# Output projection beside an attention: a tile of weights between two and two modulation tiles, split half a group ahead of its use

## The chip, the cores and the metric

The kernel runs on one core of a Trainium2 chip. The metric is device time in microseconds (us) of one launch. Before the change the median of three runs is 2190.3 us (2189.67 to 2194.18).

## What is computed

Two transformer blocks run one after the other on 256 tokens of width 2048, all in float32. The change lies in the first block, between its attention and its output projection:

```python
sh_a, sc_a, g_a, sh_m, sc_m, g_m = ada_modulation(c, w_ada, b_ada)   # silu(c) @ w_ada + b_ada, six pieces of 2048
h = modulate(rms_norm(x, norm_attn_w), sh_a, sc_a)
q, k, v, u = split_projection(h @ w_in)           # 16 query heads, 4 key heads of 64
attn = latent_window_attention(q, k, v, kc, vc, sink)
pool = multiscale_pool(u, pool_w, pool_scale)
x = x + g_a * (concat([attn, pool]) @ w_out)      # w_out: 2048 x 2048
hm = modulate(rms_norm(x, norm_mlp_w), sh_m, sc_m)
x = x + g_m * (square(relu(hm @ w_up)) @ w_down)
```

The pooled half of the concatenation (rows 1024 to 2047 of w_out) is ready before the attention; the attention's half comes later.

## The kernel before

**Split matmuls.** Every weight tile (512 rows by 512 columns, 1 MB) is loaded into a tile `raw` and split in two halves of 256 rows. For each half ACT rounds it to `wh` (line 65, called at line 174) and DVE subtracts to get the rest `wl` (line 68). A product is then three matmuls of 512 columns, `mm3` (lines 237 to 239): hi by wh, hi by wl, lo by wh. One half of a tile serves four mm3 (two k-slices by two blocks of 128 tokens).

**The list of units.** Loads and what follows them stand in one list in program order: `items` (what to load) and `units` (what to do with it). A weight tile is two units (its halves); a tile of w_ada (128 rows by 2048 columns, also 1 MB, kind `an`) is one unit: eight matmuls in the trace of line 203, which add its part of the modulation vector into the bank `adab`. `prep()` (line 161) does the next unit. `ahead(n)` (line 222) does up to n units, as long as fewer than three halves are split ahead of use and the next unit isn't held: with `state["hold"]` set, units from that number on are done by `ahead` only if they are weight halves. `take(i, h)` (line 228) gives out a half, and does units until it is there. Five `raw` tiles exist in this stage (three of `raw_p`, two extra); the load of an item starts when the item five places earlier has been used up.

**The stage.** The pooled half of the output projection is eight groups, (n, g) for n = 0..3 (512 output columns) and g = 2, 3 (512 rows). One group uses one tile: two halves, each with j = 0, 1, each with t = 0, 1, so eight mm3. Between them stand pieces of the attention: `beside(w)` (line 88) adds w to a due and steps the generator `attn1` (line 807) for each whole one. attn1 has 32 units u (one head pair member and one block of 128 queries). A unit's steps are, in the order of the program:

- scores of u: three matmuls into a bank `s` (lines 815 to 818; DVE: row maximum `mx`, line 820, and `negm`, line 821; ACT: exponential into `p`)
- in every odd unit, values of the two units before: sixteen matmuls into `o` (line 835); in every fourth unit also `esk`, `rcp`, `rw` on DVE, with a small exponential and a copy `o` on ACT
- the turn of u-1: four transposes of p into a bank `bk` (line 854), copied to `pt` by ACT (odd u) or DVE (even u, line 859)
- in every fourth unit, two transposes of rw (line 866), and DVE and ACT finish two heads (xX)

The group's loop before:

```python
for h in range(2):
    wh, wl = take(i, h, 0)
    ...
    for j in range(2):
        ahead(1)
        for t in range(2):
            mm3(...)
            beside(LP1)                  # LP1 = 1.1
        if next_kind() == "an" ...: prep(); beside(LP1 * 1.4)
while next_kind() == "an": prep(); beside(LP1 * 1.4)
ahead()
```

`ADA_POOL` (line 28) says how many w_ada tiles follow each w_out tile in the list: 6, then 4 each, the last 2. Since the next weight tile stands behind all of them, and `ahead` is held at w_ada tiles (hold is 0 in this loop), a tile's halves are split at the end of the group before, by the `ahead()` after the loop (line 913). Before the loop stands the last block of q (`in_block("q1", ...)`), which does units with no hold.

Of the kernel before, what the change touches and what calls it, by code (L numbers as in the profile page):

```python
# [24 lines left out]

CTX_AT = "q1"

FILL, ADA_IN, ADA_POOL, ADA_REST = 4, 10, (6, 4, 4, 4, 4, 4, 4, 2), 1

LP1, LAG, LAGK = 1.1, 3, 2  # L30

# [11 lines left out]
def two_blocks_kernel(ctx: ExitStack, tc: tile.TileContext, I, out: bass.AP):  # L43
# [178 lines left out]
    def ahead(n=AHEAD):  # L222
        while n and state["uw"] < min(w_used[0] + AHEAD, len(w_units)) and not (
                state["hold"] is not None and state["up"] >= state["hold"] and next_kind() != "w"):
            prep()
            n -= 1
# [8 lines left out]
    def mm3(acc, xs, wh, wl, first, last):  # L235
        hi, lo = xs
        PE.matmul(out=acc, lhsT=hi, rhs=wh, start=first, stop=False)  # L237
        PE.matmul(out=acc, lhsT=hi, rhs=wl, start=False, stop=False)  # L238
        PE.matmul(out=acc, lhsT=lo, rhs=wh, start=False, stop=last)  # L239
# [67 lines left out]
    def ada_n(n):  # L307
        for _ in range(n):
            if ada_q:
                add_direct(KINDS.pop(0) if KINDS else "an", *ada_q.popleft())  # L310
# [17 lines left out]
    def add_wo(n, g):  # L328
        wo_blk[n, g] = add_w("w", [(w_out[512 * g:512 * (g + 1), 512 * n:512 * n + 512], 0, 512)], 4, 512)

    for n in range(4):
        for g in (2, 3):
            add_wo(n, g)
            ada_n(ADA_POOL[2 * n + g - 2])
    for n in (0, 2):
        for g in (0, 1):
            for e in (0, 1):
                add_wo(n + e, g)
                ada_n(ADA_REST)
    assert not ada_q  # L340
    up_blk, down_blk, fill_unit = {}, {}, []
    for k in range(16):
# [285 lines left out]
    def in_block(nm, g, more=False):  # L628
        i = win_blk[nm, g]
        k0, n = GROUPS[g]  # L630
        who = (hx, hc) if nm == "kv" else (hx,)
        a, keys = [], []
        ws = {}
        for iw, w in enumerate(who):
            while len(w) < k0 + n:
                assert step((hp, cq)[iw])
            a += [new_acc() for _ in range(2)]
            keys += [(("kvc" if iw else nm), t) for t in range(2)]
            for h in range(2):
                if not iw:  # L640
                    ws[h] = take(i, h)
                wh, wl = ws[h]
                for j in range(n // 2):
                    for t in range(2):
                        s = slice(t * 128, (t + 1) * 128)
                        k = h * n // 2 + j
                        hi, lo = w[k0 + k]
                        mm3(a[2 * iw + t], (hi[:, s], lo[:, s]), wh[:, j], wl[:, j], k == 0, k == n - 1)
                        if more:
                            tick()  # L650
                    tick()
        for (nm_, t), ac in zip(keys, a):
            if nm_ not in proj:
                proj[nm_] = xtile("R" if nm_ in ("kv", "kvc") else "X", FP32, (128, 2, 512))
            if g == 0:
                act(proj[nm_][:, t], ac)
            else:
                V.tensor_tensor(out=proj[nm_][:, t], in0=ac, in1=proj[nm_][:, t], op=OP.add)
# [67 lines left out]
    def q_post(qb, t):  # L726
        s = slice(t * 128, (t + 1) * 128)
        rs = []
        for r in rope(proj[f"q{qb}"][:, t], 8, t, "pt"):
            rs.append(r)  # L730
            yield
        for _ in range(LAG):
            yield
        for a, r in enumerate(rs[-2:]):
            bk = bank([128, 4, 128])
            for h in range(4):
                dup_t(bk[:, h, :], r[:, h])
            q = QS[0][:, qb * 8 + 4 * a:qb * 8 + 4 * a + 4, s]
            act(q, bk)
            sub_lo(q[64:128], bk[64:128], q[64:128])  # L740
            yield
# [47 lines left out]
    QS.append(nat.tile([128, 16, 256], F32R, tag="n2", name="QS"))  # L789
    for t in range(2):  # L790
        hp.append(q_post(0, t))
    in_block("q1", LAST, True)
    while "pool" not in done:
        step(hp)
# [97 lines left out]
    for n in range(4):  # L892
        gate = None
        a = [new_acc() for _ in range(2)]
        for g in (2, 3):
            i = wo_blk[n, g]
            for h in range(2):
                wh, wl = take(i, h, 0)
                if gate is None and 2 in stored:
                    gate = gate_row(2, n)  # L900
                for j in range(2):
                    k = 4 * g + 2 * h + j
                    ahead(1)
                    for t in range(2):
                        mm3(a[t], fm(k, t), wh[:, j], wl[:, j], k == 8, k == 15)
                        beside(LP1)
                    if next_kind() == "an" and items[units[state["up"]][0]][0] == "an":
                        prep()
                        beside(LP1 * 1.4)
            while next_kind() == "an":  # L910
                prep()
                beside(LP1 * 1.4)
            ahead()
        add_gated(a, n, False, gate)
        del a

# [841 lines left out]
```

## Time and profile before

| | |
|---|---|
| median of three runs | 2190.3 us |
| the profiled execution | 2190.88 us, its span 2189.1 us |
| PE (TensorE matmul) busy | 2129.6 us, 97% of the span |
| DVE (VectorE) busy | 1221.5 us, 56% |
| ACT (ScalarE) busy | 965.8 us, 44% |
| DMA | 472.08 MB, 216 GB/s over the span |
| share of PE in the chain that ended last | 94% |

PE is the engine that works nearly all the time. What the whole-span shares hide is the stage of the attention, from about 257 to 415 us: the table of 40 slices shows PE busy 9 tenths or less there, and the clock in short stretches below full. The stage is read in the table by stretches (busy time and granted clock in each), the waits of PE (whom it waited for), and the timelines of PE, ACT and DVE (which instruction waited, and what stood ahead of it on its engine). Lines are those of the kernel before.

### The profile page before, as it was taken

To read this page: it belongs to the slowest core of one execution; us is meant where nothing else is said; L and a number is where in the kernel's file an instruction comes from. 1 tells how busy PE (TensorE), PEld (TensorE's weight loads), DVE (VectorE), ACT (ScalarE), POOL (GpSimd) and SP (SyncE) were. 2 spreads that over 40 slices of the span, in tenths; PEclk is the share of its full clock that TensorE was granted. 3 is DMA by queue.
4 is the path that set the end of the run, shared out by engine and by line. 5 is a ranking of instruction groups with operands and counts; after the bars stand their busy time and mean duration, and the time that the engine had idled before them with its cause. 6 is when DMAs were issued, how large, how long until landed. Compare 5 with 4: busy or idle time off the path is not lost.

```text
span 2189.1 us, 25717 instructions
## 1 busy us (share of the span) xinstructions
PE 2129.6 (97%) x10267; PEld 1687.2 (77%) x10267; DVE 1221.5 (56%) x1553; ACT 965.8 (44%) x1343; POOL 49.9 (2%) x90
## 2 busy tenths in 40 slices
PE   5999988999999999999999999999999999999998
PEld 3677655678888888888888887888888888888886
DVE  2455555566546656554556548746665555555554
ACT  4433333355444434443444544445544444444443
POOL 1000000010000000000001000000000000000000
PEclk9999999999999999999999999999999999999999
DMA  9988866776547867565555754554556555555553
GB/s 331 371 327 334 303 216 224 276 266 207 193 170 254 281 211 256 184 206 177 189 202 184 238 181 135 164 173 151 183 177 211 193 192 192 193 192 192 192 192 115
DMA packets 213944, 472.08 MB, mean 216 GB/s; under 512 B 8897, under 2 KB 18929, under 8 KB 204865
## 3 DMA queue, kind: packets, MB, share of 16 engines
q1 hardware_dynamic: 209312, 457.53, 61.1%
q0 software_dynamic: 4448, 12.90, 2.0%
q8 instruction: 80, 1.31, 0.2%
q14 instruction: 40, 0.32, 0.0%
q10 hardware_dynamic: 64, 0.02, 0.0%
HBM read 468.28 MB, written 4.49 MB: 216 GB/s over the span
## 4 chain that ended last, share of the span: by engine, by line
PE 94%; DVE 1%; ACT 1%; DMA 1%; issue 0%; POOL 0%; POOLq 0%; ACTq 0%; DVEq 0%
PE acc L237 28%; PE acc L238 28%; PE acc L239 28%; PE adab L203 3%; PE bk L854 1%; PE o L835 1%; PE bk L1002 1%; PE s L1253 1%; DVE wl L68 1%; DMA raw<-in_w_in_dram 1%; PE o L1296 0%; PE s L818 0%; PE bk L1197 0%; PE s L815 0%; PE bk L1343 0%; DMA raw<-in_w_ada_dram 0%
## 5 line engine op out<-in xcount | busy, mean ns | idle before, releaser
L68 DVE TENSOR_TENSOR wl<-raw,wh 128x1024 fp32r<-128x1024 f32 (+1 forms) x674 | 799.1, 1206 | 608.7 <-ACT wh L65 608.4
L65 ACT ACTIVATE wh<-raw 128x1024 fp32r<-128x1024 f32 (+1 forms) x674 | 690.3, 1043 | 526.0 <-PE acc L239 433.8
L237 PE MATMUL acc<-wh,xX 128*128 128x512 f32 x1888 | 756.9, 401 | 8.7 <-ACT wh L65 5.7
L238 PE MATMUL acc<-wl,xX 128*128 128x512 f32 x1888 | 737.9, 391 | 3.8 <-DVE wl L68 3.7
L239 PE MATMUL acc<-wh,xX 128*128 128x512 f32 x1888 | 738.6, 391 | 0.0
L237 PEld LDWEIGHTS acc<-wh,xX 128*128 128x128 f32 x1888 | 355.2, 188 | 107.5 <-issue 20.7
L239 PEld LDWEIGHTS acc<-wh,xX 128*128 128x128 f32 x1888 | 355.3, 188 | 77.3 <-DVE xX L68 0.4
L238 PEld LDWEIGHTS acc<-wl,xX 128*128 128x128 f32 x1888 | 355.9, 189 | 74.2 <-DVE wl L68 5.7
L237 PE MATMUL acc<-wh,xR 128*128 128x512 f32 x704 | 278.7, 396 | 8.0 <-ACT wh L65 8.0
L238 PE MATMUL acc<-wl,xR 128*128 128x512 f32 x704 | 275.6, 392 | 2.0 <-DVE wl L68 2.0
L239 PE MATMUL acc<-wh,xR 128*128 128x512 f32 x704 | 275.5, 391 | 0.0
L237 PEld LDWEIGHTS acc<-wh,xR 128*128 128x128 f32 x704 | 132.7, 189 | 37.1 <-ACT wh L65 8.8
L238 PEld LDWEIGHTS acc<-wl,xR 128*128 128x128 f32 x704 | 132.8, 189 | 29.4 <-DVE wl L68 3.1
L239 PEld LDWEIGHTS acc<-wh,xR 128*128 128x128 f32 x704 | 132.8, 189 | 28.0
L203 PE MATMUL adab<-raw,cst 128*32 128x512 f32 (+1 forms) x736 | 92.4, 600 | 15.8 <-DMA raw<-in_w_ada_dram 15.1
L203 PEld LDWEIGHTS adab<-raw,cst 128*32 128x32 f32 x736 | 17.6, 113 | 52.3 <-issue 27.0
L65 ACT ACTIVATE junk<-x 128x512 f32<-128x512 f32 x32 | 20.2, 631 | 66.5 <-DVE x L1097 28.7
L65 ACT ACTIVATE p<-s,negm 128x512 f32<-128x512 f32 x32 | 22.0, 688 | 61.1 <-DVE negm L821 34.7
L65 ACT ACTIVATE g<-acc,r 128x512 f32<-128x512 f32 x30 | 20.6, 690 | 55.5 <-PE acc L239 55.5
L65 ACT ACTIVATE xR<-bk 128x512 f32<-128x512 f32 (+2 forms) x26 | 13.9, 534 | 67.3 <-PE bk L1197 35.7
L820 DVE TENSOR_REDUCE mx<-s 128x1 f32<-128x512 f32 x32 | 22.1, 690 | 36.0 <-PE s L818 35.7
L65 ACT ACTIVATE r<-acc 128x512 f32<-128x512 f32 x32 | 18.8, 598 | 50.2 <-PE acc L239 39.5
(295 smaller groups left out, 1289.5 us busy)
## 6 DMA issues: line engine op xcount, KB each, us to landing
raw<-in_w_in_dram SPq DMA_DIRECT2D x151, 1024.0 KB, 5.0
raw<-in_w_ada_dram SPq DMA_DIRECT2D x88, 1024.0 KB, 6.4
raw<-in_w_mlp_up_dram SPq DMA_DIRECT2D x64, 1024.0 KB, 5.3
raw<-in_w_mlp_down_dram SPq DMA_DIRECT2D x64, 1024.0 KB, 5.0
raw<-in_w_out_dram SPq DMA_DIRECT2D x32, 1024.0 KB, 5.0
raw<-in_w_branch_dram SPq DMA_DIRECT2D x16, 1024.0 KB, 5.0
raw<-in_w_ada_dram SPq DMA_DIRECT2D x16, 512.0 KB, 8.3
raw<-in_w_in_dram SPq DMA_DIRECT2D x10, 512.0 KB, 7.3
```

The lines of the kernel that those rows point to most:

```text
L65: S.activation(out=out_, in_=in_, func=func, **kw)
L68: V.tensor_tensor(out=lo, in0=full, in1=hi.bitcast(FP32), op=OP.subtract)
L203: PE.matmul(out=accs[key][32 * j:32 * j + 32, :], lhsT=cst[:, 4 * k + j if kind == "ak" else k, :], rhs=r[:, j, :], start=k == 0, stop=k = ...
L237: PE.matmul(out=acc, lhsT=hi, rhs=wh, start=first, stop=False)
L238: PE.matmul(out=acc, lhsT=hi, rhs=wl, start=False, stop=False)
L239: PE.matmul(out=acc, lhsT=lo, rhs=wh, start=False, stop=last)
L820: V.tensor_reduce(out=mx, in_=s, axis=AX.X, op=OP.max)
L835: PE.matmul(out=ob[pair_][64 * e:64 * e + 64, 0, t, :], lhsT=vn[j][:, g * 64:(g + 1) * 64], rhs=pb[w - 1 + e][:, j, :], start=j == 0, stop ...
L854: PE.transpose(bk[:, j, :], p[:, j * 128:(j + 1) * 128], ident)
L1002: PE.transpose(bk[:, j, t * 128:(t + 1) * 128], rs[t][:, (2 * pr + j) * 128:(2 * pr + j + 1) * 128], ident)
L1253: PE.matmul(out=s[:, i, :], lhsT=QT[nm][p, h, t * 128:(t + 1) * 128], rhs=KT[nm][p, h, 0:nk], start=True, stop=True)
```

## The change

In the list of units each w_out tile of the pooled half now has two w_ada tiles ahead of it and two behind it, so four lie between two tiles (two between the first and the second). `ADA_POOL` becomes 2. The number of units after the first w_out tile is kept as `wo_units`, and `hold` is set to it before the block of q1, so that w_ada tiles behind that one are left for the groups. In the loop `ahead(1)` is called before each mm3 instead of before each pair, one w_ada tile is done after each pair, and the loop over left-over w_ada tiles and the `ahead()` at a group's end are gone. With four w_ada tiles between two weight tiles, the next tile's halves come up after two of them: before the third pair of the group (j = 0 of the second half), one half before each of its two mm3. The four w_ada tiles per group, and the total, stay. The last six w_ada tiles stand 2, 1, 1, 1, 1 behind the first tiles of the attention's half, where they stood 1 each.

```diff
-FILL, ADA_IN, ADA_POOL, ADA_REST = 4, 10, (6, 4, 4, 4, 4, 4, 4, 2), 1
+FILL, ADA_IN, ADA_POOL, ADA_REST = 4, 10, 2, 1
...
     for n in range(4):
         for g in (2, 3):
+            ada_n(ADA_POOL)
             add_wo(n, g)
-            ada_n(ADA_POOL[2 * n + g - 2])
+            if n + g == 2:
+                wo_units = len(units)
+            else:
+                ada_n(ADA_POOL)
+    ada_n(ADA_POOL)
     for n in (0, 2):
         for g in (0, 1):
             for e in (0, 1):
                 add_wo(n + e, g)
-                ada_n(ADA_REST)
+                ada_n(ADA_POOL if n + g + e == 0 else ADA_REST)
...
     for t in range(2):
         hp.append(q_post(0, t))
+    state["hold"] = wo_units
     in_block("q1", LAST, True)
...
                 for j in range(2):
                     k = 4 * g + 2 * h + j
-                    ahead(1)
                     for t in range(2):
+                        ahead(1)
                         mm3(a[t], fm(k, t), wh[:, j], wl[:, j], k == 8, k == 15)
                         beside(LP1)
-                    if next_kind() == "an" and items[units[state["up"]][0]][0] == "an":
+                    if next_kind() == "an":
                         prep()
                         beside(LP1 * 1.4)
-            while next_kind() == "an":
-                prep()
-                beside(LP1 * 1.4)
-            ahead()
         add_gated(a, n, False, gate)
         del a
```

How the order of instructions moves is shown at three places. In the names, mx, negm, p, pt, o, rw are those of the attention above; QS is the queries' tile; lines after the change are higher by 6 or 7.

**Place 1, DVE, the split of tile (1, 3).** Before, at the end of group (1, 2):

```order
L867 TENSOR_TENSOR o<-o 128x256
L68 TENSOR_TENSOR xX<-o,xX 128x256
L820 TENSOR_REDUCE mx<-s 128x1
L821 TENSOR_SCALAR negm<-mx,sink_140 128x1
L68 TENSOR_TENSOR wl<-raw,wh 128x1024 x2
L820 TENSOR_REDUCE mx<-s 128x1
L821 TENSOR_SCALAR negm<-mx,sink_140 128x1
L859 COPY pt<-bk 128x512
```

With the change, from the third pair of group (1, 2):

```order
L852 COPY rw<-rcp 128x256
L68 TENSOR_TENSOR wl<-raw,wh 128x1024
L827 TENSOR_REDUCE mx<-s 128x1
L828 TENSOR_SCALAR negm<-mx,sink_140 128x1
L68 TENSOR_TENSOR wl<-raw,wh 128x1024
L866 COPY pt<-bk 128x512
L874 TENSOR_TENSOR o<-o 128x256
L68 TENSOR_TENSOR xX<-o,xX 128x256
```

The two wl stood in a row, ahead of the maximum of the next scores; now they stand apart with one maximum between them, and the copy pt of a turn stands behind the second.

**Place 2, ACT, the same tile.** Before:

```order
L65 ACTIVATE p,psum__1919<-s,negm 128x512
L65 ACTIVATE xX<-o 128x256
L65 ACTIVATE p,psum__1919<-s,negm 128x512
L65 ACTIVATE pt<-bk 128x512
L65 ACTIVATE wh<-raw 128x1024 x2
L65 ACTIVATE p,psum__1919<-s,negm 128x512 x2
```

With the change:

```order
L65 ACTIVATE esk<-esk 128x4
L65 ACTIVATE o<-o 128x256
L65 ACTIVATE pt<-bk 128x512
L65 ACTIVATE wh<-raw 128x1024
L65 ACTIVATE p,psum__1913<-s,negm 128x512
L65 ACTIVATE wh<-raw 128x1024
L65 ACTIVATE xX<-o 128x256
L65 ACTIVATE p,psum__1913<-s,negm 128x512
```

The two wh stood in a row behind a pt; now an exponential p stands between them.

**Place 3, DVE, the split of tile (1, 2) and the first scores.** Before:

```order
L68 TENSOR_TENSOR QS<-bk,QS 64x4x128 x2
L820 TENSOR_REDUCE mx<-s 128x1
L821 TENSOR_SCALAR negm<-mx,sink_140 128x1
L820 TENSOR_REDUCE mx<-s 128x1
L821 TENSOR_SCALAR negm<-mx,sink_140 128x1
L820 TENSOR_REDUCE mx<-s 128x1
L821 TENSOR_SCALAR negm<-mx,sink_140 128x1
L68 TENSOR_TENSOR wl<-raw,wh 128x1024 x2
```

With the change, from group (0, 3):

```order
L699 TENSOR_TENSOR dup<-xX,rm 128x512 x2
L68 TENSOR_TENSOR wl<-raw,wh 128x1024
L68 TENSOR_TENSOR QS<-bk,QS 64x4x128
L68 TENSOR_TENSOR wl<-raw,wh 128x1024
L68 TENSOR_TENSOR QS<-bk,QS 64x4x128
L827 TENSOR_REDUCE mx<-s 128x1
L828 TENSOR_SCALAR negm<-mx,sink_140 128x1
L827 TENSOR_REDUCE mx<-s 128x1
```

The split came after three maxima; now its halves stand between the last parts of the queries (QS), ahead of the first maximum.

## Rows read from the trace of the kernel before

**Rows 1.** The first line of the page's chain of waits that ended last: shares of the span by engine.

```profile
PE 94%; DVE 1%; ACT 1%; DMA 1%; issue 0%; POOL 0%; POOLq 0%; ACTq 0%; DVEq 0%
```

**Rows 2.** The table by stretches, three stretches between 250 and 410 us (the last lies within the second). Columns: the stretch and its length, then busy us and instruction count of PE, PEld, DVE, ACT and POOL, then PEclk (the granted TensorE clock, 1.00 being full speed), the DMA share and GB/s.

```profile
250.00:270.00 20.00, 18.49 (x106) 10.63 (x106) 13.94 (x23) 6.08 (x9) 2.56 (x5) 1.00 0.93 335
270.00:410.00 140.00, 121.10 (x794) 76.87 (x793) 70.87 (x145) 54.08 (x116) 1.62 (x3) 0.91 0.67 227
300.00:310.00 10.00, 7.55 (x43) 4.29 (x42) 4.93 (x8) 3.31 (x6) 0.00 (x0) 0.83 0.66 214
```

**Rows 3.** The waits of PE between 250 and 440 us: who was waited for, us in total, times, longest us.

```profile
PE acc L237 <- ACT wh L65: 13.6, 6, 2.9
PE acc L238 <- DVE wl L68: 5.7, 7, 1.4
PE bk L854 <- ACT p L65: 1.0, 1, 1.0
PE o L866 <- DVE rw L845: 0.3, 1, 0.3
```

**Rows 4.** The timeline of PE. Columns: start in us, duration in us (a matmul's duration overlaps the next, so pitch is read from start to start), engine, line, operation, out<-in, shape, count, and in brackets the idle time before it with its releaser.

```profile
258.92 0.50 PE L238 MATMUL acc<-wl,xX 128*128 128x512 f32 x1 [1.43 <-DVE wl L68]
...
273.00 0.66 PE L854 MATMUL bk<-ident,p 128*128 128x128 f32 x4 [1.03 <-ACT p L65]
...
301.80 0.50 PE L237 MATMUL acc<-wh,xX 128*128 128x512 f32 x1 [1.69 <-ACT wh L65]
303.06 0.50 PE L238 MATMUL acc<-wl,xX 128*128 128x512 f32 x1 [0.76 <-DVE wl L68]
...
308.41 0.45 PE L818 MATMUL s<-xR,QS 128*128 128x512 f32 x1
...
319.99 0.39 PE L237 MATMUL acc<-wh,xX 128*128 128x512 f32 x1
...
320.68 0.60 PE L854 MATMUL bk<-ident,p 128*128 128x128 f32 x4
...
328.11 0.92 PE L854 MATMUL bk<-ident,p 128*128 128x128 f32 x4
...
332.44 0.66 PE L854 MATMUL bk<-ident,p 128*128 128x128 f32 x4
...
341.99 1.09 PE L835 MATMUL o<-pt,xR 128*64 128x128 f32 x16
343.01 0.50 PE L237 MATMUL acc<-wh,xR 128*128 128x512 f32 x1
...
343.83 0.60 PE L854 MATMUL bk<-ident,p 128*128 128x128 f32 x4
344.18 0.48 PE L237 MATMUL acc<-wh,xR 128*128 128x512 f32 x1
...
344.96 0.40 PE L815 MATMUL s<-xR,QS 128*128 128x512 f32 x1
...
345.63 1.07 PE L203 MATMUL adab<-raw,cst 128*32 128x512 f32 x8
346.63 0.66 PE L854 MATMUL bk<-ident,p 128*128 128x128 f32 x4
```

**Rows 5.** The timeline of ACT, same columns.

```profile
270.87 1.28 ACT L65 ACT_TABLE_LOAD   x1 [1.80 <-DVE negm L821]
272.16 0.69 ACT L65 ACTIVATE p<-s,negm 128x512 f32<-128x512 f32 x1
...
275.32 0.69 ACT L65 ACTIVATE p<-s,negm 128x512 f32<-128x512 f32 x1 [1.04 <-DVE negm L821]
...
276.00 1.99 ACT L65 ACTIVATE wh<-raw 128x1024 fp32r<-128x1024 f32 x2
...
300.21 0.60 ACT L65 ACTIVATE pt<-bk 128x512 f32<-128x512 f32 x1 [0.80 <-PE bk L854]
300.70 1.99 ACT L65 ACTIVATE wh<-raw 128x1024 fp32r<-128x1024 f32 x2
...
309.95 0.69 ACT L65 ACTIVATE p<-s,negm 128x512 f32<-128x512 f32 x1 [3.71 <-DVE esk L840]
...
311.31 0.60 ACT L65 ACTIVATE pt<-bk 128x512 f32<-128x512 f32 x1 [0.21 <-PE bk L854]
...
324.82 0.19 ACT L65 ACTIVATE esk<-esk 128x4 f32<-128x4 f32 x1
```

**Rows 6.** The timeline of DVE, same columns.

```profile
277.08 2.36 DVE L68 TENSOR_TENSOR wl<-raw,wh 128x1024 fp32r<-128x1024 f32 x2 [1.87 <-ACT wh L65]
...
308.90 0.69 DVE L820 TENSOR_REDUCE mx<-s 128x1 f32<-128x512 f32 x1 [1.75 <-PE s L818]
309.62 0.21 DVE L821 TENSOR_SCALAR negm<-mx,sink 128x1 f32<-128x1 f32 x1
...
325.45 0.29 DVE L845 COPY rw<-rcp 128x256 f32<-128x256 f32 x1
```

**Rows 7.** The timeline of SP's DMA issues (SPq; start in us, then the time from the first issue to the end of the last of a merged row), the issues of two tiles of w_out; and the page's line on all of w_out's loads (count, KB each, median us from issue to landing).

```profile
260.03 0.38 SPq L152 DMA_DIRECT2D raw<-in_w_out_dram  x1
...
279.47 0.38 SPq L152 DMA_DIRECT2D raw<-in_w_out_dram  x1
...
raw<-in_w_out_dram SPq DMA_DIRECT2D x32, 1024.0 KB, 5.0
```

## The prediction

> **What bounds the kernel now.** I read the page's chain of waits first: 94% of the span is PE's own work [rows 1], so time comes off only where PE stands still or runs slowly. The table by stretches shows where that is: from 270 to 410 us, the attention beside the pooled half of the output projection, PE is busy 121.1 of 140 us and the granted clock is 0.91 on the mean, while before 270 it is 1.00 [rows 2]. The waits of PE name the cause: 13.6 us in six waits for ACT's `wh`, 5.7 us in seven waits for DVE's `wl`, 1.0 us for the first exponential `p`, and 0.3 us for `rw`, which I leave as it is [rows 3]. So seven of the eight groups begin with a wait for their own tile: one short (1.43 us for wl, at 258.92), six with both parts, the least of them 1.69 + 0.76 = 2.45 us at 301.80 and 303.06 [rows 4]. Together 20.3 us.
>
> The cause is order, not supply. The tile of 276.00 was sent for at 260.03, and a w_out load takes 5.0 us at the median, so it lay there from about 265 [rows 7]; its `wh` began at 276.00, 0.68 us after the exponential that stands ahead of it on ACT began [rows 5].
>
> **The clock.** [...] After the one near 327 us, PE needs 4.33 us from the turn at 328.11 to that at 332.44; the same four kinds of work (turn, mm3, scores, w_ada tile) take 2.80 us from 343.83 to 346.63, at full clock [rows 4]. That is 1.5 us per drop. The table agrees from above: a stretch with one drop has 0.83, which is 1.7 us of 10, and 140 us at 0.91 are 12.6 us, or some seven such drops for the six waits [rows 2]. Part of that fell into idle time, so I count 7 x 1.5 = 10.5 us. The wait of 1.43 us was followed by none, its stretch is at 1.00 [rows 2, 4]; the shortest that one follows has 2.45 us. The stage loses 20.3 + 10.5 = 30.8 us.
>
> **The change, part by part.** No arithmetic is added or removed: as many w_ada tiles, w_out halves and attention steps. What moves is the place of the splits: half a group (four mm3) ahead. The seven waits for wh and wl as such go, since a half is then asked for some 9 us after it was put into the queues. But a half still stands in the queues of ACT and DVE, which also carry the attention, and what is behind it there comes later. So I followed each new split by the pitches of the rows:
>
> - PE: mm3 0.75 us (0.69 from 319.99 to 320.68, 0.82 from 343.01), turn 0.35, w_ada tile 1.0, values 1.02 [rows 4]. Scores take 0.67 ahead of a w_ada tile [rows 4]; ahead of other work, where the next starts before they end, I take 0.6. The rw transposes are taken as 0.14, two against a turn's four. These last two are estimates.
> - The last matmul of the scores to mx 0.49 (308.41 to 308.90), so 0.89 from their first, which starts 0.4 earlier (an estimate from the 0.67); mx to negm 0.72, negm to p 0.33 [rows 4 to 6].
> - p to the next ACT instruction 0.68; turn to pt 0.69; pt to wh 0.49; two wh in 1.99; wh to wl 1.08; two wl in 2.36, so 1.18 each [rows 5, 6]. A pt on DVE is taken as 0.69, like the mx of as many columns [rows 6].
>
> *Tile (1, 3), places 1 and 2.* Count from the turn of unit 4. pt 0.69, wh 1.18, wl 2.26 to 3.44. Behind that wl on DVE stands the maximum of unit 6: mx 3.4, negm 4.1, p 4.45. Behind that p on ACT stands the second wh 5.1; wl 6.2 to 7.4; and behind that on DVE the pt of unit 5, done at 8.05. The values need that pt. PE reaches them after turn, mm3, scores, mm3, turn, w_ada, rw, scores, mm3: 0.35 + 0.75 + 0.6 + 0.75 + 0.35 + 1.0 + 0.14 + 0.6 + 0.75 = 5.3. It waits **2.8 us**. Here the wait for a weight turns into a wait for a pt.
>
> *Tile (1, 2), place 3.* Counted from the last queries' transposes, ACT does wh at 0.1 and QS at 1.05, DVE wl to 2.3, QS to 3.0, mx, negm 3.7; then the table load and p at 5.3 (1.29 from the load to p), the turn at 6.1 (0.84 from p) [rows 4, 5]. PE is there after 0.35 + 1.0 + 0.6 + 0.6 + 0.75 = 3.3: **2.8 us**, where it was 1.0.
>
> *Tile (2, 3).* One exponential stands between the halves, and then esk and rw. From the scores of unit 16: mx 0.9, negm 1.6, p 1.9, wh 2.6, wl 3.7 to 4.9, mx 4.8, p 5.9, wh 6.6, wl 7.65 to 8.8, esk on ACT 9.0, rw 0.63 later (324.82 to 325.45), done 0.3 after that [rows 5, 6], so its transposes 10.0. PE's own way is 0.6 + 0.35 + 0.75 + 0.6 + 0.75 + 1.02 + 1.0 + 0.35 + 0.6 + 0.75 + 0.35 + 0.75 = 7.9: **2.1 us**.
>
> *The other four.* (2, 2): two wh in a row, two wl in a row, pt at 7.6, PE there at 7.5: 0.1 us. (3, 2): a pt between the two wl, done at 5.55 (wh 2.6, wl 3.7 to 4.9, pt 0.69) against 4.2: 1.4 us. (3, 3): a pt between the two wh, so wl to 6.35, mx 6.3, negm 7.0, pt to 7.85, against 6.8: 1.1 us. (0, 3): ahead of the attention, beside the queries' transposes: none.
>
> Sum: 2.8 + 2.8 + 2.1 + 0.1 + 1.4 + 1.1 = 10.3 us of idle. Two of these are past 2.45 us and cost a drop; 2.1 is nearer to 2.45 than to 1.43, so a third; 1.4 and 1.1 cost none: 3 x 1.5 = 4.5 us. After: 14.8 us. **Gain 30.8 - 14.8 = 16.0 us.** The profiled execution is 2190.88 us, 0.6 above the median of 2190.3; 2190.9 - 16.0 = **2175 us**. Unknown are the waits behind the queues. From below, none of them: 30.8 us gained, 2160. From above, each as dear as a wait now: nothing gained, 2191.
>
> Loads are covered: the stage moves 227 GB/s at a DMA share of 0.67; 16 us less of 140 makes 227 x 140 / 124 = 256 GB/s, against 335 at a share of 0.93 in the 20 us ahead [rows 2]. If that cover went, each microsecond of a late tile is one of PE. The moved w_ada tiles behind the attention's half stand beside full PE work before and after; the hold leaves one w_ada tile fewer in q1's block and one more in the first group, 1.0 us either way, nothing on the sum.
>
> [...]
>
> **The rivals.** *All waits go* (2160): attention instructions become ready later or the chains run shorter than I add up; the waits are 1.1 to 2.8 us, sums of five to ten pitches, and none was seen in this order. Against it: place 1's chain has no slack to find. *Moved in full* (2187, within 0.2%): all six tiles from (1, 2) on go like (1, 3), 6 x 2.8 = 16.8 us, with the seven drops, 10.5: 27.3 us in place of 30.8. For it: ACT and DVE are shared with the softmax in every group; against it: two halves stand in a row at (2, 2), and (3, 2) and (3, 3) have one pt between. *Slower, by supply*: a tile is wanted half a group earlier, and if its load isn't there, `wh` stops ACT with every p behind it. Today a tile is sent for at 279.47 and split at 300.70, 16 us after its landing [rows 5, 7]; half of a 24.7 us group (276.00 to 300.70) earlier leaves 4. It decides once a load takes over 9 us in place of 5.0; at 13 us each of six tiles loses 4 us, 24 in all, past the 16.0: 2199. Against it: the load's start depends on the tile before, which is used up earlier too. That the change doesn't do what it says is excluded: the order on DVE and ACT shows the halves split there.
>
> **How the numbers follow.** My sum, give or take 6 us (2169 to 2181): 0.60. All waits go: 0.13. A gain of only 5 to 12 us, with drops after 1.4 and 1.1 us too: 0.11. Moved in full: 0.11. Slower: 0.05. A measurement of this kernel tells 0.2%, 4.4 us, from no change; faster by more are the first three, 0.84, same 0.11, slower 0.05. The range of 2163 to 2185 leaves out the last two, a little of the third, and the low end of the second.
>
> **What would show it.** In the changed profile the waits of PE for wh and wl from 250 to 420 us fall from 19.3 us to under 2; new ones stand at the values (for pt, on DVE), at rw's transposes and at the first turn (for p), 10 us together, the longest near 2.8; the stretch from the first scores to the end of (3, 3) has two or three drops in place of seven; the DMA rate there is near 256 GB/s. Wrong it would be if PE waits on w_ada or w_out loads, if waits for wh stay, or if stretches at 0.83 stand behind waits near 1 us.

## The result, and the profile after

The changed kernel takes 2173.15 us, the median of five runs (2171.35 to 2173.7); the kernel before, run beside it, 2190.82. The ratio is 0.9912, interval [0.990, 0.9923]. The forecast was 2175 in a range of 2163 to 2185. The profiled execution took 2173.7 us, its span 2171.9, so 17.2 us less than the profiled one of before.

Page, chain that ended last, shares by engine, which answers to [rows 1]:

```profile
PE 94%; DVE 1%; ACT 1%; DMA 0%; issue 0%; POOL 0%; POOLq 0%; ACTq 0%; DVEq 0%
```

The bound is PE as before. The waits of PE between 250 and 440 us, the query of [rows 3]:

```profile
PE o L842 <- DVE pt L866: 2.8, 3, 2.1
PE bk L861 <- ACT p L65: 2.6, 1, 2.6
PE o L873 <- ACT pt L65: 1.8, 1, 1.8
PE bk L710 <- ACT rows L65: 0.8, 1, 0.8
PE o L873 <- ACT o L65: 0.5, 1, 0.5
```

No wait for `wh` or `wl` is left: 19.3 us of them are gone. In their place stand 8.5 us of other waits, at the places that the forecast named (values for `pt`, the first turn for `p`, the transposes of `rw`) and one that it did not (`rows`). The timeline of PE, the rows with these waits but the last (0.54 us at 392.43) and two rows more; each wait stands in the brackets, a duration overlaps the next row:

```profile
256.94 1.06 PE L203 MATMUL adab<-raw,cst 128*32 128x512 f32 x8
258.78 0.63 PE L710 MATMUL bk<-ident,dup 128*128 128x128 f32 x4 [0.77 <-ACT rows L65]
...
272.88 0.66 PE L861 MATMUL bk<-ident,p 128*128 128x128 f32 x4 [2.56 <-ACT p L65]
...
277.02 0.93 PE L861 MATMUL bk<-ident,p 128*128 128x128 f32 x4
...
295.84 1.09 PE L842 MATMUL o<-pt,xR 128*64 128x128 f32 x14 [2.11 <-DVE pt L866]
...
337.95 0.41 PE L873 MATMUL o<-ident,rw 128*128 128x128 f32 x2 [1.81 <-ACT pt L65]
...
356.73 1.09 PE L842 MATMUL o<-pt,xR 128*64 128x128 f32 x14 [0.54 <-DVE pt L866]
...
378.37 1.09 PE L842 MATMUL o<-pt,xR 128*64 128x128 f32 x14 [0.17 <-DVE pt L866]
```

In the order of the forecast: first turn 2.56 us (tile (1, 2)), values 2.11 (1, 3), none listed (2, 2), rw transposes 1.81 (2, 3), 0.54 (3, 2), 0.17 (3, 3). A bracket counts from the recorded end of the matmul ahead, which lies behind the moment when the next could start (the one at 292.51 is recorded with 0.39 us, and the next starts 0.23 us after it, at 292.74), so it is shorter than the time lost. Read from start to start, PE loses 2.73, 2.54, 0.30, 1.97, 0.97 and 0.60 us at these six places. At (1, 3), for instance, the values begin at 293.30 and the next mm3 at 296.86, 3.56 us later where 1.02 is usual [rows 4]; at (2, 2) the sixteen values of 316.54 show no wait, but the next start comes 1.32 us later (317.86). Two of the releasers named here ended within 0.1 us of another: those transposes of 337.95 read DVE's `rw` (337.51, 0.29), the ones of 258.78 DVE's `dup` (the first of two from 257.94, 0.6 each).

The table by stretches, columns as in [rows 2]:

```profile
250.00:270.00 20.00, 19.23 (x116) 10.69 (x114) 16.21 (x25) 7.86 (x11) 2.55 (x5) 1.00 0.98 354
270.00:410.00 140.00, 132.16 (x903) 84.08 (x902) 80.20 (x163) 59.38 (x124) 2.16 (x4) 0.98 0.78 270
270.00:280.00 10.00, 7.44 (x46) 4.36 (x44) 4.34 (x10) 4.11 (x8) 0.00 (x0) 0.83 0.88 314
340.00:350.00 10.00, 10.00 (x73) 6.75 (x75) 3.90 (x9) 3.45 (x11) 0.00 (x0) 0.88 0.63 231
```

In the 140 us from 270, PE is busy 132.2 us where it was 121.1, and the granted clock is 0.98 where it was 0.91. Two stretches of low clock are left in them: behind the waits of 2.56 us (0.66 from 273 to 278 us) and 1.81 us (0.66 from 338 to 343). The 2.11 us of 295.84 are followed by none (1.00 from 295 to 305).

The chain behind one of the two longest predicted waits, that of (1, 3), on ACT and on DVE (same columns as [rows 5, 6]):

```profile
288.43 0.60 ACT L65 ACTIVATE pt<-bk 128x512 f32<-128x512 f32 x1 [0.25 <-PE bk L861]
288.92 1.05 ACT L65 ACTIVATE wh<-raw 128x1024 fp32r<-128x1024 f32 x1
292.20 0.69 ACT L65 ACTIVATE p<-s,negm 128x512 f32<-128x512 f32 x1 [2.23 <-PE o L873]
...
292.88 1.05 ACT L65 ACTIVATE wh<-raw 128x1024 fp32r<-128x1024 f32 x1
```

```profile
290.01 1.22 DVE L68 TENSOR_TENSOR wl<-raw,wh 128x1024 fp32r<-128x1024 f32 x1 [1.58 <-ACT wh L65]
291.15 0.68 DVE L827 TENSOR_REDUCE mx<-s 128x1 f32<-128x512 f32 x1
291.87 0.21 DVE L828 TENSOR_SCALAR negm<-mx,sink 128x1 f32<-128x1 f32 x1
293.96 1.23 DVE L68 TENSOR_TENSOR wl<-raw,wh 128x1024 fp32r<-128x1024 f32 x1 [1.88 <-ACT wh L65]
295.10 0.68 DVE L866 COPY pt<-bk 128x512 f32<-128x512 f32 x1
```

The second `wl` (293.96) waited for a `wh` (292.88) behind an exponential (292.20) that needed the `mx` of 291.15, which stood behind the first `wl` (290.01). The bracket of that exponential names PE's transposes of `rw`, which ended at 292.10, 0.02 us behind the `negm` that it reads (291.87, 0.21). The `pt` of 295.10 is behind all of them, and the values of 295.84 need it: 8.17 us from the turn of 287.67, where the forecast had 8.1.

The supply, answering to [rows 7] (issues of w_out tiles on SP's queue, and the page's line on all w_out loads):

```profile
255.47 0.38 SPq L152 DMA_DIRECT2D raw<-in_w_out_dram  x1
...
268.33 0.38 SPq L152 DMA_DIRECT2D raw<-in_w_out_dram  x1
...
raw<-in_w_out_dram SPq DMA_DIRECT2D x32, 1024.0 KB, 5.1
```

The tile of 268.33 is split at 288.92, 20.6 us later. The tightest is that of 255.47, split from 261.07, 5.6 us later against a load of 5.1 at the median; its `wh` shows no wait for it, and between 250 and 395 us no `wh` waits for a load at all.

**Where the gain lies.** From the first queries' matmuls (219.54 before, 220.22 after) to the end of the projections (469.29 and 450.06) the changed kernel is 19.9 us shorter. About 2 of these are given back at the next place. The timeline of PE there, after:

```profile
450.06 0.60 PE L935 MATMUL bk<-ident,x 128*128 128x128 f32 x4
...
456.83 0.68 PE L970 MATMUL rsb<-dg,ones 128*128 128x128 f32 x4 [1.14 <-DVE dg L969]
458.83 0.80 PE L237 MATMUL acc<-wh,xX 128*128 128x512 f32 x1 [1.32 <-ACT xX L65]
```

The wait of 1.32 us was there before, that of 1.14 was not, and the matmul at 458.83 runs at the low clock (0.80 us; the clock is 0.57 from 458 to 462). From the last gated add to rsb it takes 5.67 us in both kernels (469.32 to 474.99, 451.16 to 456.83); but that add begins 0.03 us after the end of the projections before, and 1.10 us after it now, behind a `wl` of the MLP's first tile (449.74 to 450.97) and the load of its gate, which lands 0.2 us later.

### The profile page after: what moved, and what is told of

Same layout as the page of the kernel before. It is cut to its first block, busy times and chain, and to the rows that moved or that the text cites. A ratio compares the mean times of both kernels' runs of the same rounds, so it can differ in the third digit from the quotient of the medians.

```text
span 2171.9 us, 25718 instructions
## 1 busy us (share of the span) xinstructions
PE 2123.6 (98%) x10267; PEld 1683.9 (78%) x10267; DVE 1220.3 (56%) x1553; ACT 964.6 (44%) x1343; POOL 49.8 (2%) x90
## 4 chain that ended last, share of the span: by engine, by line
PE 94%; DVE 1%; ACT 1%; DMA 0%; issue 0%; POOL 0%; POOLq 0%; ACTq 0%; DVEq 0%
PE acc L237 28%; PE acc L239 28%; PE acc L238 28%; PE adab L203 3%; PE o L842 1%; PE bk L861 1%; PE bk L1005 1%; PE s L1256 1%; PE o L1299 0%; PE bk L1200 0%; ACT wh L65 0%; PE s L822 0%; PE bk L1346 0%; PE s L825 0%; DMA raw<-in_w_ada_dram 0%
## 5 line engine op out<-in xcount | busy, mean ns | idle before, releaser
L237 PEld LDWEIGHTS acc<-wh,xX 128*128 128x128 f32 x1888 | 355.8, 188 | 99.7 <-issue 19.5
L237 PEld LDWEIGHTS acc<-wh,xR 128*128 128x128 f32 x704 | 132.2, 188 | 29.0 <-issue 2.5
L65 ACT ACTIVATE g<-acc,r 128x512 f32<-128x512 f32 x30 | 20.6, 690 | 55.5 <-PE acc L239 55.5
L65 ACT ACTIVATE v<-bk 128x512 f32<-128x512 f32 x32 | 19.2, 600 | 48.0 <-PE bk L1005 48.0
```

Of the source, the lines that this page charges most:

```text
L65: S.activation(out=out_, in_=in_, func=func, **kw)
```

## The experiments

Theory: the lead of half a group is the gain, and what is left of waits are chains of halves and attention steps that stand in a row on ACT and DVE. Rivals: the gain comes from something else in the change (loop, hold); the load on ACT and DVE, or the supply, sets the waits that are left. The kernel before ran beside each group of runs (2192.75, 2192.34 and 2191.99 us in the median), so the ratios are compared.

| kernel | us, median | ratio to before | waits of PE, 250 to 420 us |
|---|---|---|---|
| the changed kernel, first time | 2173.15 | 0.9912 [0.990, 0.9923] | 8.5 |
| the changed kernel, again | 2171.84 | 0.9912 [0.9898, 0.9926] | 8.5 |
| no lead, split behind the gated add | 2204.09 | 1.0052 [1.0039, 1.0064] | 25.8 |
| no lead, split ahead of the gated add | 2198.52 | 1.0028 [1.0018, 1.0038] | 22.3 |
| lead of a quarter group | 2173.77 | 0.9916 [0.9903, 0.993] | 8.8 |
| lead of three quarters | 2171.67 | 0.9904 [0.9891, 0.9918] | 7.0 |
| no hold of q1's block | 2176.57 | 0.9928 [0.9915, 0.994] | 11.6 |
| halves in a row | 2168.39 | 0.9887 [0.9874, 0.9901] | 5.8 |
| table of the exponential early | 2170.16 | 0.9896 [0.9881, 0.9911] | 7.2 |
| both of these | 2166.19 | 0.9881 [0.9868, 0.9895] | 4.5 |
| both, and the end of the projection | 2176.82 | 0.9932 [0.9919, 0.9944] | as both |

### The lead taken away

```diff
-            ada_n(ADA_POOL)
+            ada_n(4 if n + g > 2 else 2)
             add_wo(n, g)
...
-            else:
-                ada_n(ADA_POOL)
-    ada_n(ADA_POOL)
+            elif n + g < 6:
+                ada_n(0)
+    ada_n(len(ada_q) - 6)
```

> The changed kernel with all four w_ada tiles ahead of a w_out tile and none behind it (the first two tiles excepted), so that its halves are split at the end of the group before, with the new loop kept. Theory: the lead of half a group is the whole gain. Waits of PE for wh and wl come back at the head of the groups, 10 to 19 us between 250 and 420 us, with five to seven stretches of low clock: 2186 to 2192 us. Rival, the gain comes from the loop (a split before each mm3, one w_ada tile after each pair, the hold of q1's block): the waits for wh and wl stay under 5 us and the time is 2172 to 2180 us.

It took 2204.09 us: slower than the kernel before by 0.5%, beyond what either theory had. The waits for wh and wl are back, 14.5 and 9.4 us. Two of them in the timeline of PE:

```profile
281.20 0.49 PE L237 MATMUL acc<-wh,xR 128*128 128x512 f32 x1 [1.29 <-ACT wh L65]
284.48 0.79 PE L238 MATMUL acc<-wl,xR 128*128 128x512 f32 x1 [2.79 <-DVE wl L68]
```

A wait of 2.79 us for wl does not occur before (0.76 is usual in [rows 4]); here it does at two groups. In the new loop nothing is split at a group's end, so where a gated add follows, its four instructions stand ahead of the `wl` on DVE (timeline of DVE of this kernel):

```profile
280.56 0.68 DVE L891 TENSOR_TENSOR o<-acc,g 128x512 f32<-128x512 f32 x1
...
282.60 0.69 DVE L892 TENSOR_TENSOR x<-x,o 128x512 f32<-128x512 f32 x1
283.21 2.35 DVE L68 TENSOR_TENSOR wl<-raw,wh 128x1024 fp32r<-128x1024 f32 x2
```

So it undid more than the lead, and a second kernel puts the split ahead of the gated add again:

```diff
                         prep()
                         beside(LP1 * 1.4)
+            ahead()
         add_gated(a, n, False, gate)
```

> The kernel with all four w_ada tiles ahead of a w_out tile, as in the earlier run that came out 11 us slower than the kernel before, but with the split at the group's end put ahead of the gated add again, as in the kernel before; the loop and the hold of q1's block stay as in the changed kernel. Theory: in the earlier run the wait of 2.8 us for wl behind the gated add (four instructions of 0.7 us on DVE) and the low clock behind it, at three of the groups, made the excess over the kernel before; the lead alone is the rest. So the time is the kernel before's within 3 us (ratio 0.9985 to 1.0015) and the waits for wh and wl sum to 18 to 21 us. Rival: the new loop or the hold is worth several microseconds by itself, up or down: ratio under 0.997 or over 1.003.

2198.52 us, 1.0028. The waits of PE from 250 to 420 us, the two largest:

```profile
PE acc L237 <- ACT wh L65: 14.5, 7, 2.9
PE acc L238 <- DVE wl L68: 5.0, 7, 0.8
```

They sum to 19.5 us as the theory had them, yet the time is 6.5 us above the kernel before, where it allowed 3; the rival's ratio of over 1.003 lies inside the interval. In the profiled executions some 5 us of it can be placed: 1.6 us are lost ahead of the stage (its first matmuls of the queries stand at 221.13 against 219.54, and PE's waits for w_ada loads ahead of 250 us sum to 16.3 us against 15.1), all waits from 250 to 420 us are 22.3 us against 20.6, and the stretch 250 to 270 has a clock of 0.91 where it was 1.00, 1.8 us of 20. Some 1.4 us stay open. What follows: with the new loop and the hold but no lead nothing is gained, and in this loop the lead is worth the difference to the changed kernel, some 25 us. The lead in the loop of before was not run.

### Another lead

```diff
-            ada_n(ADA_POOL)
+            ada_n(3 if n + g > 2 else 2)
             add_wo(n, g)
...
+            elif n + g < 6:
+                ada_n(1)
+    ada_n(len(ada_q) - 6)
```

> The changed kernel with three w_ada tiles ahead of a w_out tile and one behind it, so that the halves are split before the fourth pair, a quarter of a group ahead. Theory: what is needed is the lead of one chain of split (some 4.4 us from the first wh to the second wl, plus what stands ahead of it on ACT and DVE), and a quarter group is some 5.5 us: the wait for wh and wl stays away or is under 3 us in sum, and the waits behind the queues move to other places with about the same sum, 5 to 11 us: 2172 to 2180 us. Rival, each group needs half a group of lead because ACT and DVE are 3 us late on the mean: waits for wl of 1 to 1.5 us in most of the groups, some 8 us, and drops of the clock behind them: 2180 to 2186 us.

> The changed kernel with one w_ada tile ahead of a w_out tile and three behind it, so that the halves are split before the second pair of a group, three quarters of a group ahead. Theory (any lead of a quarter group or more will do, and what is left is where the halves fall among maxima, exponentials and copies): no waits for wh and wl, other waits of 4 to 12 us in sum at other places, 2168 to 2178 us. Rival 1 (the lead counts, half a group is not yet enough): fewer waits than the 8.5 us of the changed kernel, and 2165 to 2170 us. Rival 2 (supply): a tile is wanted 5.5 us earlier and its load is late for some; PE or ACT waits for the DMA of w_out, and the time is 2178 us or more.

2173.77 us for a quarter group and 2171.67 for three quarters (1 and 3 in place of 3 and 1 in the diff): both the changed kernel's time within its interval, both as the theory had it. Neither has a wait of PE for wh, wl or a load there. So the lead has to exist; how long it is hardly counts here. What is left merely changes places. In the quarter group three scores wait for a `p` (3.4 us in sum), which they do in none of the others, and one mm3 has a wait of which only the second kernel without lead shows a small case (0.42 us, at 334.47). In PE's timeline:

```profile
322.45 0.50 PE L237 MATMUL acc<-wh,xR 128*128 128x512 f32 x1 [3.02 <-DVE o L891]
```

Here the first mm3 of the next output columns wants the bank that the gated add still reads, and this add (321.71) stood on DVE behind a `wl` (319.53), esk, rcp and rw.

### Halves in a row

```diff
                 for j in range(2):
                     k = 4 * g + 2 * h + j
+                    ahead(2)
                     for t in range(2):
-                        ahead(1)
                         mm3(a[t], fm(k, t), wh[:, j], wl[:, j], k == 8, k == 15)
```

> The changed kernel with both halves of a tile split in a row before the third pair of the group (half a group ahead, as now), not one before each of the pair's two mm3. Theory: the waits that are left (2.1 us for pt at (1, 3), 1.8 us at the rw transposes of (2, 3)) come from the halves standing apart on ACT and DVE, each behind an exponential or a maximum. In a row they are done as one chain of two wh and two wl, the pt of (1, 3) comes some 2 us earlier, and the two waits fall from 3.9 us to under 1.5 us; with the clock stretch behind the second gone (1.5 us), the time is 2168 to 2171 us against 2173.2 of the changed kernel. Rival 1, the lead and the load on ACT and DVE set the waits, not the interleaving: the four values and turns wait 3.5 to 5 us in sum as now, 2172 to 2175. Rival 2, a row of two wl (2.36 us) holds the maximum of the next scores and stops PE at the turn for p: a new wait of 1 to 2 us in some groups, 2174 to 2180.

2168.39 us, ratio 0.9887 against 0.9912: as the theory had it. DVE and PE at (1, 3) in this kernel:

```profile
287.00 2.36 DVE L68 TENSOR_TENSOR wl<-raw,wh 128x1024 fp32r<-128x1024 f32 x2 [1.58 <-ACT wh L65]
289.28 0.68 DVE L827 TENSOR_REDUCE mx<-s 128x1 f32<-128x512 f32 x1
290.00 0.21 DVE L828 TENSOR_SCALAR negm<-mx,sink 128x1 f32<-128x1 f32 x1
290.13 0.68 DVE L866 COPY pt<-bk 128x512 f32<-128x512 f32 x1
```

```profile
284.67 0.66 PE L861 MATMUL bk<-ident,p 128*128 128x128 f32 x4
...
290.30 1.66 PE L842 MATMUL o<-pt,xR 128*64 128x128 f32 x16
```

From the turn the `pt` begins 5.46 us later where it was 7.43 (287.67 to 295.10), and the values show no wait; their sixteen matmuls take 1.66 us where 1.09 are usual [rows 4], so up to 0.6 us is still inside them. The waits of PE from 250 to 420 us in this kernel:

```profile
PE bk L861 <- ACT p L65: 2.7, 2, 1.9
PE o L842 <- DVE pt L866: 1.7, 1, 1.7
PE bk L710 <- DVE dup L699: 0.9, 1, 0.9
PE o L873 <- ACT o L65: 0.5, 1, 0.5
```

At (2, 3) the 1.81 us at the rw transposes became 0.74 us at the turn for `p`, a wait as rival 2 had it but smaller; at (3, 2) the 0.54 us became 1.68, since both `wl` now stand ahead of its `pt`; the first turn waits 1.91 us in place of 2.56. In sum 5.8 us are listed in place of 8.5. The execution profiled was the fastest of its four (2165.77), and from 250 to 400 us it has no stretch of low clock (1.00 from 250 to 270 and in each 10 us behind it). That the load on ACT and DVE sets the waits (rival 1) is ruled out: both engines do the same work (DVE is busy 1219.0 us here and 1220.3 in the changed kernel, ACT 964.7 and 964.6).

### The table of the exponential

```diff
     state["hold"] = wo_units
+    act(warm, half_neg[:, 0:1], AF.Exp)
     in_block("q1", LAST, True)
```

> The changed kernel with one exponential of a single column on ACT ahead of q1's block, whose result nobody uses; ACT's load of the exponential's table (1.28 us, at 270.75) then stands there and not between the first negm and the first p. Theory: the wait of 2.56 us at the first turn lies on the chain of ACT, so it falls by the table load to 1.3 us, and if the low clock behind it (0.83 from 270 to 280 us) hangs on the length of that wait it goes too: 1.3 to 2.8 us off, 2170.3 to 2172 us. Rival, the load comes back, since a copy or a rounding between the two takes another table, or the first p waits for negm and not for ACT: the wait stays at 2.3 to 2.6 us, 2173 us.

2170.16 us, a ratio of 0.9896, 3.5 us below the changed kernel's by the ratios, whose intervals overlap; the theory had 1.3 to 2.8. PE's first turn:

```profile
272.09 0.66 PE L862 MATMUL bk<-ident,p 128*128 128x128 f32 x4 [1.29 <-ACT p L65]
```

2.56 became 1.29 us: the load of the table, now at 235.59 on ACT, was on the path in full, and none of the `wh`, `QS` and `rows` between it and the first `p` (271.26) brought it back. The stretch from 270 to 280 us ran at a clock of 1.00.

> The changed kernel with both edits that helped alone: the halves split in a row, and the exponential's table loaded ahead of q1's block. Theory: the two take away different waits (the pt of (1, 3) and the rw of (2, 3); the table at the first turn), so the gains add: 4.8 us and 3.0 us less than the changed kernel, 2165.5 us of 2173.2, or 2164 to 2167. Rival: in the row order the first turn waits 1.91 us and no longer for the table alone but for the two wl ahead of the queries' last part on DVE; then the table's 1.28 us hide and the second edit gives 0 to 1 us more: 2167.5 to 2169.

Both edits together: 2166.19 us against 2171.84 of the changed kernel in the same group, the fastest of all kernels run. The waits add as the theory had them: the first turn waits 0.63 us, 1.28 less than with the row alone (1.91). The time is 1.3 us below the row alone by the ratios. That is the size of the wait, but the intervals of the two overlap widely. Of the second edit's 3.5 us (3.0 in the theory) only the idle part came again; the row kernel's profile shows no low clock there to win back (1.00 from 270 to 280 us).

### The clock, from one kernel run twice

> The changed kernel itself, run beside the others of this group so that differences of two or three microseconds are read from one chip. All theories: a ratio to the kernel before of 0.990 to 0.9923 as at first, some 17 to 21 us less than the kernel before.

2171.84 us and a ratio of 0.9912, as at first. Its profile beside the first one tells more than its time: the same program, the same waits, other drops. PE in this second profile, at the three long waits:

```profile
272.79 0.66 PE L861 MATMUL bk<-ident,p 128*128 128x128 f32 x4 [2.56 <-ACT p L65]
...
275.65 0.66 PE L861 MATMUL bk<-ident,p 128*128 128x128 f32 x4
...
294.21 1.09 PE L842 MATMUL o<-pt,xR 128*64 128x128 f32 x14 [2.10 <-DVE pt L866]
...
337.92 0.41 PE L873 MATMUL o<-ident,rw 128*128 128x128 f32 x2 [1.80 <-ACT pt L65]
```

From the first turn to the next it takes 2.86 us here, and 4.14 in the first profile (272.88 to 277.02): full clock here, the lower level there (from 270 to 280 us 1.00 here, 0.83 there). The two executions are 0.09 us apart at the first turn, 1.63 at the values, 0.03 at the rw transposes and 1.53 at the next values (355.20 against 356.73). So the first execution lost 1.54 us behind the first wait and 1.50 behind the third, the second one 1.60 behind the second wait alone (0.83 from 290 to 300 us, where the first has 1.00). A drop costs 1.5 to 1.6 us, and which of three waits of 1.8 to 2.6 us has one changes from execution to execution.

### The hold

```diff
-    state["hold"] = wo_units
     in_block("q1", LAST, True)
```

> The changed kernel without the hold of q1's block, so that one w_ada tile more is done in that block and one fewer is left for the groups; the halves then come up at other pairs. Theory (the prediction's: the hold puts nothing on the sum): no waits for wh and wl, the waits that are left change their places, 6 to 11 us in sum, and the time is the changed kernel's within 3 us, 2170 to 2176. Rival: the hold keeps the w_ada tiles that give the groups their lead, and without it one or two groups lose the lead: waits for wh or wl of 2.5 us and a drop of the clock each, 2177 to 2182 us.

2176.57 us, just outside the theory's range, and 3.5 us above the changed kernel by the ratios, whose intervals overlap. The rival is wrong too: no wait for wh or wl. The waits sum to 11.6 us, 3.1 more than in the changed kernel, and lie at other places, four for `pt` (5.2 us, the longest 2.37), three for `p` (3.1) and one of 2.0 at the rw transposes: without the hold the halves come up at other pairs.

### The end of the projection

```diff
-    def gate_row(chunk, n):
-        g = b1.tile([128, 512], FP32, tag="gt", name="g", bufs=1)
+    def gate_row(chunk, n, tag="gt"):
+        g = b1.tile([128, 512], FP32, tag=tag, name="g", **({"bufs": 1} if tag == "gt" else {}))
...
-            wh, wl = take(i, h)
+            wh, wl = take(i, h, last)
...
-                    gate = gate_row(2, n + e)
+                    gate = gate_row(2, n + e, "rm" if e else "gt")
...
+                         last=0 if n + e + g == 4 else AHEAD)
```

The last line is 0 for the last tile of w_out alone: there `take` splits no half ahead.

> The kernel with both edits, and the end of the output projection freed: the gate of every second tile goes into another buffer, so that its load need not wait for the gated add before, and in the last tile of w_out no half of the MLP's first tile is split ahead of its gated add. Theory: of the gain in the attention some 2 us are given back where PE waits for dg at rsb (1.14 us in the changed kernel, none before), since the last gated add stands behind a wl and behind its gate's load; with both gone that wait goes to 0.2 us or less and the time falls by 0.9 us, or by 2.4 us where a stretch of low clock stood behind it. Rival: the halves that are split later are then missing at the head of the MLP (three halves, 2.2 us each from wh to wl), PE waits there for wh or wl instead, 1 to 3 us: no gain, or 1 to 2 us slower.

2176.82 us against 2166.19 without these edits: 10.6 us slower, the rival's direction and five times its price. The waits of PE from 440 to 475 us:

```profile
PE bk L936 <- DVE x L893: 4.3, 2, 2.4
PE acc L237 <- ACT wh L65: 2.6, 1, 2.6
PE rsb L972 <- DVE dg L971: 0.9, 1, 0.9
...
```

The gate's load still came late: the other buffer is one that the gated add itself writes, and the last add waited 3.99 us for it (DVE at 445.50). The next five up tiles were sent for only at 460.45 (451.00 in the changed kernel), and the DMA moved 27 and 10 GB/s in the two stretches from 440 to 460 us. The likely reason is that halves held back do not use up the MLP's first tiles, and a load waits for a tile to be used up; the two edits were not run apart. What of the 1.14 us at rsb is due to the `wl` and what to the gate, it does not tell; that stays open.

## Why the prediction was right, and where its sizes were off

**The waits for wh and wl.** Forecast gone (under 2 us left), measured gone. Right. The kernels without lead have them again.

**(1, 3), 2.8 us: measured 2.11 in the bracket, 2.54 from start to start.** The chain was right to 0.1 us (8.17 against 8.1). PE's own way was the term that was off: it reached the values at 293.30, 5.63 us after the turn, not 5.3, and ran two of the sixteen. Half of that is the turn ahead of the w_ada tile, which takes 0.53 us (290.13 to 290.66) and was summed at 0.35. The rest of the gap to 2.11 is the measure: the forecast adds up pitches, which are starts.

**(1, 2), 2.8 us: measured 2.56, by starts 2.73.** The chain was followed in its pieces, with the table load on it; taking the load away gave 1.27 us, its whole duration.

**(2, 3), 2.1 us: 1.81, by starts 1.97. (2, 2), 0.1: none, 0.30. (3, 2), 1.4: 0.54, 0.97. (3, 3), 1.1: 0.17, 0.60.** The places are right. The chains on ACT and DVE ended within 0.1 us of the forecast at (2, 3), (3, 2) and (3, 3) too (10.07 us from the first scores to the rw transposes, against 10.0; 5.49 and 7.81 to the end of the pt, against 5.55 and 7.85); PE's own way took 8.1, 4.58 and 7.26 us where 7.9, 4.2 and 6.8 were summed. The sum came to 7.2 us in brackets and 9.1 by starts, in place of 10.3.

**(0, 3), none: 0.77 us.** Not foreseen, and the same mechanism: the `wl` that are split there (255.07 and 256.81) stand on DVE ahead of the `dup` of 257.94, which the transposes of 258.78 read. Before, the `dup` were done at 257.7, ahead of the `wl`, and PE waited 1.43 us for a `wl` instead [rows 4]. The 0.5 us for ACT's `o` near 392 were 0.3 for `rw` before.

**The clock.** Forecast three drops of 1.5 us; two in the first profile, one in the second, at 1.5 to 1.6 us each. The price was right. It was read behind the wait near 327 us, which has two parts in the timeline of PE before:

```profile
326.28 0.50 PE L237 MATMUL acc<-wh,xR 128*128 128x512 f32 x1 [2.21 <-ACT wh L65]
327.54 0.50 PE L238 MATMUL acc<-wl,xR 128*128 128x512 f32 x1 [0.76 <-DVE wl L68]
```

Behind it and the five other long waits of before the clock is low: over the 5 us from 278, 303, 328, 351, 376 and 400 us it is 0.50, 0.66, 0.66, 0.66, 0.66 and 0.67. The rule behind the count, that a drop follows waits of about 2.1 us and more, was not: 2.56 us had one in one execution and none in the other, 1.8 us likewise, and 2.1 us the other way round.

**The sum.** The 30.8 and the 14.8 of the forecast are not of one measure: the 20.3 us of waits before are brackets, the 10.3 after are starts. Read from start to start, less the usual pitch of the same two instructions, the fourteen waits from 250 to 410 us before come to some 22.8 us (an estimate; 301.80 to 303.06, for one, is 1.26 us, 0.92 over the usual pitch of 0.34, where the bracket says 0.76). So with all other terms kept the forecast was a gain of some 18.5 in the stage, not 16.0. The waits after are 10.6 us by starts, with the two that were not foreseen, which takes 0.3 off, and one drop fewer gives 1.5: some 19.7, and the positions give 19.9. The whole shows 17.2, since about 2 us went at rsb (1.14 us of wait and a low clock behind it), which no step of the forecast looked at. Misses in opposite directions, then: 3.9 us more in the stage than the 16.0, 2 less behind it, 0.7 at its start. The 2175 came out nearer than its terms, and that part is luck: 3.9 us too few in the stage stand against 2.7 lost outside it.

**The hold at nothing.** Wrong, by 3.5 us in the ratios and by 3.1 us in the waits listed: it adds no work, but it decides at which pair the halves come up.

**The order on ACT and DVE.** The 10.3 us take the instructions of each engine in the order of the program, and the trace agrees: nothing on DVE passed the blocked `wl` of 293.96 in the 1.88 us that DVE stood idle ahead of it, with a `pt` behind it whose transposes PE had ended long before (290.13, duration 0.60). Removing what stood between the halves left at most 0.6 us of the wait. The rivals: *all waits go* had none left, and 8.5 us of listed waits remain; *moved in full* had 2.8 us at each of six tiles, and the six have 0 to 2.56 in brackets, 0.30 to 2.73 by starts; *slower by supply* was far off, with 20.6 us between issue and split for the tile worked out and DMA at 270 GB/s (forecast 256) in the stage.

## What to carry to other kernels

When a conversion on a helper engine is what the main engine waits for at each tile, give it a lead; a quarter of a group did as much as three quarters here (0.9916 and 0.9904), and in neither did PE wait for a half. Then look at what the conversion now stands between: where what stands behind a blocked instruction waits with it, as the copy `pt` did here behind the `wl` of 293.96 (DVE idle for 1.88 us), two halves with a softmax step between them make one chain out of two, and keeping them together was worth some 5 us more than placing each ahead of its own matmul. A move that adds no work, such as the hold here, still decides at which instructions the two queues meet, and so which waits are left; they are read from the order, tile by tile. And a sum of pitches is compared with waits that are read from start to start, before and after alike.

## What was not expected of the hardware

The same program with the same waits had its low clock stretches at other places in two executions (behind the first and third wait, or behind the second alone), each costing 1.50 to 1.60 us. In other kernels of this study waits of 1.91 us (halves in a row, at 271.40) and 2.37 us (no hold, at 329.72) were followed by full clock (1.00 from 270 to 280 and from 330 to 340 us), while the first turn of the kernel with a lead of three quarters waits 1.9 us too and has the lower level behind it (0.83 from 270 to 280 us). Length of a wait alone does not tell whether a drop follows; what does was not found by these runs.

The load of the exponential's table, 1.28 us, was on PE's path in full, and one instruction of a single column placed 35 us ahead took it off; at 235.59 it cost nothing that the profile shows: from PE's first matmuls of the queries (220.71) to the transposes of 259.27 it takes 38.56 us, as in the changed kernel (220.22 to 258.78). Of PE's wait 1.27 us went, the length of the load, and ACT had stood idle ahead of it (2.55 us in the changed kernel, 1.80 before, [rows 5]).
